# A two-layer decoder trunk on one core: four heads' values of one attention run in a row with the next four heads' scores, their results in the sums' banks, the second attention two units sooner

## The chip, the cores and the metric

The kernel runs on one core of one Trainium2 chip. A core has a matrix engine (TensorE, PE in the profile; its weight loads are listed as PEld), VectorE (DVE), ScalarE (ACT), GpSimd (POOL) and a queue engine (SyncE, SP), which here issues nearly all transfers. TensorE writes to PSUM, an accumulator memory of eight banks of 128 partitions by 512 float32; ScalarE and VectorE read it from there into SBUF. The metric is the device time of one execution in microseconds. Before the change it is 841.62 us, the median of three runs (841.48 to 841.85).

## The reference

The input is `x` of 1 x 256 x 1024 in float32, through two layers and a final RMSNorm. A layer adds a mixer of three gated branches and then a squared-ReLU MLP:

```
h = rms_norm(x, attn_norm[l])
p = h @ w_in                      # split into cq, ckv, k_rope, mq, mk, mv, rq, rk, rv, rg, three gates
o_mla  = mla_branch(...)          # 8 heads, causal attention, head size 96 for scores and 64 for values
o_moba = moba_branch(...)         # 8 heads of 64; one block of 256 keys, so it is causal attention too
o_ret  = retention_branch(...)    # 4 heads, decay matrix, group norm, silu(g)
merged = sigmoid(g_mla) * (o_mla @ w_branch_mla) + ... + sigmoid(g_ret) * (o_ret @ w_branch_ret)
x = x + merged @ w_out
x = x + square(relu(rms_norm(x, mlp_norm[l]) @ w_mlp_up)) @ w_mlp_down
```

Each attention head needs scores of 256 queries by 256 keys, a softmax over the causal part, and the product of the probabilities with the values.

## The kernel before

**Products.** The weights arrive as float32 in pieces of up to 128 x 1024. `fetch` (L180) lets ScalarE round each piece to a high part `whi` (L191) and VectorE form the rest `wlo` (L193); activations are split in the same way. A product is the sum of three matmuls, `three` (L211 to L214), each with 128 x 512 results as a rule. The attention's own products take unsplit float32, which the profile shows as two matmul records each.

**Units and steps.** The work of a layer's mixer is a list `prog` of units, most of them 24 matmuls with one piece pair of weights: `project` (L324) makes four units for each 512 columns of `w_in`, and `branch` (L487) four units for each branch's output product. `at(slot, step)` hangs a small step (transposes, scores, values) behind a unit. Counted from the unit "mv 3", which is 0, the units are: gate of MLA 1 to 8, gate of MoBA 9 to 16, MLA's output product 17 to 20, `rqk` 21 to 24, `rv` 25 to 28, `rg` 29 to 32, MoBA's output product 33 to 36, then the retention's gate.

**The first attention (MLA).** Its heads' scores (L750) stand at units 0 to 7, one head a unit, the turning of the probabilities (`turn`, L419: three transposes into `ps_pt`, and a ScalarE copy to `probT`) two units later, and `values` (L437) for heads 0 to 3 at unit 6 and for heads 4 to 7 at unit 10.

**The second attention (MoBA).** `first` is unit 12 (L762). `moba_turn` (L766) transposes two heads' queries and keys into `pqk`, which ScalarE copies (`copied_pair`, L384). `four` (L464) makes four heads' scores by `together` (L373) and their softmax, at units 12 and 21 (`GAP` is 9); the turning stands 3 and 4 units behind that, `values` 5 units behind, at 17 and 26.

**Parts of the array.** A head of the second attention has 64 rows, so `together` gives two heads to the two halves of the array's rows (tile 64 x 128 in the profile: `64*128`). `values` gives two heads to the two halves of the columns (`128*64`). The retention's scores (`ret_scores`, L812, unit 28) run through `together` as well, behind `ret_turn` (L802, units 26 and 27). All other matmuls take the whole array (`128*128`).

**Banks.** PSUM has four banks under the tag `acc`, for the sums of projections and branches (two at a time), and four under `misc` for all else, among them `values`' result `po`, which `split_plain` (L230) reads by ScalarE (high part) and VectorE (low part).

**Order.** Each engine runs its list strictly in order and waits at semaphores. The lists are written at build time by a planner that runs the program in a timing model of its own and moves instructions of one engine past each other where data allow. Only inside `tc.manual_schedule(engines={PE})` the written order of TensorE's instructions holds among themselves. In the kernel before, `together` and `values` have such a block each.

Of the kernel before, what the change touches and what calls it, by code (L numbers as in the profile page):

```python
# [7 lines left out]
F32 = mybir.dt.float32  # L8
# [6 lines left out]
P = 128  # L15
D = 1024
S = 256
# [111 lines left out]
def trunk(ctx: ExitStack, tc: tile.TileContext, gx, wts, consts, gfin, gn, xtok, out):  # L129


    nc = tc.nc
# [4 lines left out]
    sb = ctx.enter_context(tc.tile_pool(name="sb", bufs=1))  # L137
# [8 lines left out]
    DEC = cp.tile([P, K_END - K_DEC], F32, name="DEC")  # L146
# [55 lines left out]
    def misc_tile(name="misc"):  # L202
        return ps.tile([P, 512], F32, name=name, tag="misc", bufs=4)
# [4 lines left out]
    def t4(name):  # L208
        return sb.tile([P, 4, S], F32R, name=name, tag="t4", bufs=T4)
# [20 lines left out]
    def split_plain(src, hi, lo):  # L230
        nc.scalar.activation(hi, src, AF.Copy)
        nc.vector.tensor_sub(lo, src, hi.bitcast(F32))
# [126 lines left out]
    def rope(xv, c0, s0, t, n, h, w=None):  # L359
# [10 lines left out]
        nc.vector.tensor_sub(xv[:, :, 0, :], av[:, :, 0, :], bv[:, :, 1, :])  # L370
        nc.vector.tensor_add(xv[:, :, 1, :], av[:, :, 1, :], bv[:, :, 0, :])

    def together(parts, heads):  # L373

        with tc.manual_schedule(engines={mybir.EngineType.PE}):
            for banks, a, b in heads:
                for o, sa, sb_ in parts:
                    for j, bank in enumerate(banks):  # L380
                        rows = slice(64 * j, 64 * j + 64)
                        nc.tensor.matmul(bank[:, o], a[rows, sa], b[rows, sb_], start=True, stop=True)  # L382

    def copied_pair(pt):  # L384

# [4 lines left out]
    def attention_head(score, scale):  # L390


        got = {}

        def scores(s_ps=None):
            if s_ps is None:
                s_ps = misc_tile("ps_s")
                score(s_ps[:, 0:P], slice(0, P), slice(0, P))
                score(s_ps[:, P : 3 * P], slice(P, S), slice(0, S))
            p = sb.tile([P, 3 * P], F32, name="prob", bufs=4)  # L400
            m = small("smx")
# [12 lines left out]
            nc.vector.reciprocal(m[:, 6:8], m[:, 4:6])  # L414
            for i, (a, b) in enumerate(spans):
                nc.vector.tensor_scalar(p[:, a:b], p[:, a:b], m[:, 6 + i : 7 + i], None, op0=ALU.mult)
            got["p"] = p

        def turn():  # L419
            pt = misc_tile("ps_pt")  # L420
            for i, src in enumerate((0, P, 2 * P)):
                nc.tensor.transpose(pt[:, P * i : P * i + P], got["p"][:, src : src + P], ident)  # L422
            pT = sb.tile([P, 3 * P], F32, name="probT", bufs=5)
            nc.scalar.activation(pT, pt[:, : 3 * P], AF.Copy)
            return pT

        return scores, turn

    def attention(oT, score, vs, scale, first, group=None):


        pT = {}

        def turned(h, turn):
            pT[h] = turn()

        def values(h0):  # L437


            o, v = misc_tile("po"), vs()  # L440
            with tc.manual_schedule(engines={mybir.EngineType.PE}):
                for h in (h0 + 2, h0):
                    cs = slice(S * (h - h0) // 2, S * (h - h0) // 2 + S)
                    for i in range(2):
                        for j in (1, 0):
                            vh = v[i][:, VD * (h + j) : VD * (h + j) + VD]
                            dst = o[64 * j : 64 * j + 64, cs]
                            if i == 0:
                                nc.tensor.matmul(dst, vh, pT[h + j][:, 0:S], start=True, stop=False)  # L449
                            else:  # L450
                                nc.tensor.matmul(dst[:, P:S], vh, pT[h + j][:, S : 3 * P], start=False, stop=True)  # L451
            split_plain(o, *(part[:, h0 // 2 : h0 // 2 + 2, :].rearrange("p k s -> p (k s)") for part in oT))

        heads = [attention_head(lambda o, qs, ks, h=h: score(h, o, qs, ks), scale) for h in range(8)]
        for h, (scores, turn) in enumerate(heads):
            if group is None:
                at(first + h, scores)
                at(first + h + 2, lambda h=h, turn=turn: turned(h, turn))
                if h % 4 == 3:
                    at(first + h + 3, lambda h=h: values(h - 3))  # L460
        if group is None:
            return

        def four(h0):  # L464
            for h, bank in enumerate(group(h0), h0):
                heads[h][0](bank)

        for i in range(2):
            at(first + GAP * i, lambda i=i: four(4 * i))
            for h in range(4):  # L470
                at(first + GAP * i + 3 + h // 2, lambda h=4 * i + h: turned(h, heads[h][1]))
            at(first + GAP * i + 5, lambda i=i: values(4 * i))

    def gates(l, key, xn):

# [98 lines left out]
    def layer(l, xn, before):  # L574

        c0 = []
        c, mla, mqkv, rqkv = {}, {}, {}, {}
# [164 lines left out]
        omlaT, omobaT, oretT = [], [], []  # L742
# [9 lines left out]
        attention(  # L752
            omlaT, mla_score,
            lambda: mla["v"], QKD**-0.5, first,
        )

        th_moba = gates(l, "gmoba", xn)
        merged, mT = {}, ([], [])  # L760
        branch(l, "bmla", omlaT, th_mla, merged)
        first = slot("gmoba0", 3)  # L762
        at(first, lambda: omobaT.extend((t4("omobah"), t4("omobal"))))
        qkT = {}

        def moba_turn(i):  # L766
            pt = misc_tile("pqk")
            for a, key in enumerate(("mq", "mk")):
                for t in range(NT):
                    nc.tensor.transpose(  # L770
                        pt[:, (2 * a + t) * P : (2 * a + t + 1) * P], mqkv[key][t][:, P * i : P * i + P], ident
                    )
            qkT[i] = copied_pair(pt)
# [8 lines left out]

        for i in range(4):
            at(first + 4 * (i // 2) - 3 + i % 2, lambda i=i: moba_turn(i))
        attention(omobaT, None, lambda: mqkv["mv"], MB_D**-0.5, first, moba_scores)

# [13 lines left out]
        rT, or_ps, aT, rg, oret = [], [], {}, {}, []  # L800

        def ret_turn(i):  # L802
            pt = misc_tile("prt")
            for a in range(2):
                for t in range(NT):
                    nc.tensor.transpose(
                        pt[:, (2 * a + t) * P : (2 * a + t + 1) * P],
                        rqkv["rqk"][t][:, 256 * a + P * i : 256 * a + P * i + P], ident,
                    )
            rT.append(copied_pair(pt))  # L810

        def ret_scores():  # L812
            banks = [misc_tile("ps_r") for _ in range(RT_H)][::-1]
            together(
                ((slice(0, S), slice(0, P), slice(0, S)), (slice(S, 3 * P), slice(P, S), slice(P, S))),
                [(banks[2 * i : 2 * i + 2], rT[i][1], rT[i][0]) for i in range(2)],
            )
            for h in range(RT_H):
                aT[h] = sb.tile([P, 3 * P], F32, name="retA", tag="prob", bufs=4)
                nc.vector.tensor_mul(aT[h], banks[h][:, : 3 * P], DEC[:, 384 * h : 384 * h + 384])  # L820

        def ret_values(h):
            if h == 0:
# [259 lines left out]
        for t in range(NT):  # L1083
# [3 lines left out]
            for half in range(2):  # L1087
                cs = slice(512 * half, 512 * half + 512)
# [35 lines left out]
FIRST = 4  # L1124
WHOLE = 1
AHEAD = 1
GAP = 9
T4 = 9


# [73 lines left out]
```

## Time and profile before

| What | Value |
|---|---|
| median of three runs | 841.62 us |
| the profiled execution itself | 841.8 us, its span 840.0 us |
| TensorE matmuls | 833.3 us busy, 99% of the span, 4454 records |
| VectorE | 575.0 us, 68% |
| ScalarE | 491.4 us, 59% |
| GpSimd | 27.9 us, 3% |
| DMA | 151.10 MB, 180 GB/s on the mean |

A matmul's row in the timeline has its start, its duration, line and tiles. Matmuls overlap in the pipeline, so a row lasts longer than the time to the next start, and what one costs is read from start to start; of a row that merges several records only the first start is shown. Times in the timeline count from the start of the span.

### The profile page before, as it was taken

Reading aid. Unit: us, or ns where it says so; the run is one execution under the profiler, and the core shown is the slowest. Engines: PE = TensorE matmul, PEld = TensorE weight load, DVE = VectorE, ACT = ScalarE, POOL = GpSimd, SP = SyncE. Lnnn points to the kernel's source line nnn. Section 1 sums busy time; section 2 is a strip of 40 time slices with the busy share of each in tenths; the row PEclk is TensorE's granted clock in tenths of the full one; section 3 lists DMA queues with packets and bytes.
Section 4 is the critical chain, followed back from the end, with each engine's and each line's share of the span. In section 5 each row is a group of like instructions: output and inputs, shape, how many; then the busy total and the mean of one; then the engine's idle time right before and its main releaser. Section 6 shows DMA issues by size and latency. Waiting matters only on the chain.

```text
span 840.0 us, 12183 instructions
## 1 busy us (share of the span) xinstructions
PE 833.3 (99%) x4454; PEld 708.6 (84%) x4454; DVE 575.0 (68%) x1088; ACT 491.4 (59%) x860; POOL 27.9 (3%) x31
## 2 busy tenths in 40 slices
PE   9999999999999999999999999999999999999997
PEld 7888877888998888888888887788889988888886
DVE  6887568596777666666589865675968666666663
ACT  7757666445556555555677666564556555555552
POOL 0000000040000000000000000001300000000000
PEclk9999999999999999999999999999999999999999
DMA  9755544546456665656366545554665556666641
GB/s 343 272 202 185 175 136 147 160 131 215 144 177 222 199 190 190 194 187 190 114 212 211 178 137 174 148 159 145 178 207 165 170 187 197 200 185 193 194 130 51
DMA packets 43115, 151.10 MB, mean 180 GB/s; under 512 B 4912, under 2 KB 5936, under 8 KB 43056
## 3 DMA queue, kind: packets, MB, share of 16 engines
q1 hardware_dynamic: 42480, 149.66, 56.4%
q8 instruction: 35, 0.57, 0.3%
q10 hardware_dynamic: 576, 0.67, 0.2%
q14 instruction: 24, 0.20, 0.1%
HBM read 149.26 MB, written 1.05 MB: 179 GB/s over the span
## 4 chain that ended last, share of the span: by engine, by line
PE 99%; DVE 0%; ACT 0%; issue 0%; DVEq 0%
PE acc L212 20%; PE acc L214 20%; PE acc L213 20%; PE pup L979 13%; PE pup L981 7%; PE acc L930 5%; PE ps_pt L422 1%; PE ps_s L750 1%; PE po L449 1%; PE ps_s L382 1%; PE acc L643 1%; PE acc L644 0%; PE pqk L770 0%; PE acc L646 0%; PE warm L554 0%; PE po L451 0%
## 5 line engine op out<-in xcount | busy, mean ns | idle before, releaser
L193 DVE TENSOR_TENSOR wlo<-raw,whi 128x1024 fp32r<-128x1024 f32 (+4 forms) x287 | 337.9, 1185 | 192.4 <-ACT whi L191 134.8
L191 ACT ACTIVATE whi<-raw 128x1024 fp32r<-128x1024 f32 (+4 forms) x287 | 292.3, 1023 | 188.2 <-PE acc L214 101.3
L212 PE MATMUL acc<-whi,xs 128*128 128x512 f32 (+1 forms) x384 | 151.8, 397 | 0.0
L213 PE MATMUL acc<-wlo,xs 128*128 128x512 f32 (+1 forms) x384 | 150.5, 392 | 0.0
L214 PE MATMUL acc<-whi,xs 128*128 128x512 f32 (+1 forms) x384 | 149.5, 390 | 0.0
L979 PE MATMUL pup<-xs,whi 128*128 128x512 f32 x496 | 121.3, 390 | 0.0
L979 PEld LDWEIGHTS pup<-xs,whi 128*128 128x128 f32 x496 | 92.4, 188 | 18.8
L212 PE MATMUL acc<-whi,sq 128*128 128x512 f32 x256 | 100.1, 391 | 0.0
L213 PE MATMUL acc<-wlo,sq 128*128 128x512 f32 x256 | 99.9, 390 | 0.0
L214 PE MATMUL acc<-whi,sq 128*128 128x512 f32 x256 | 99.0, 389 | 0.0
L212 PEld LDWEIGHTS acc<-whi,xs 128*128 128x128 f32 x384 | 72.1, 188 | 15.2 <-issue 1.3
L214 PEld LDWEIGHTS acc<-whi,xs 128*128 128x128 f32 x384 | 72.1, 188 | 14.3
L213 PEld LDWEIGHTS acc<-wlo,xs 128*128 128x128 f32 x384 | 72.2, 188 | 13.4
L981 PE MATMUL pup<-xs,wlo 128*128 128x256 f32 x496 | 68.3, 283 | 0.0
L981 PEld LDWEIGHTS pup<-xs,wlo 128*128 128x128 f32 x496 | 65.6, 191 | 2.8
L990 ACT ACTIVATE relu<-relu 128x256 f32<-128x256 f32 x64 | 25.8, 410 | 57.1 <-DVE relu L989 57.1
L214 PEld LDWEIGHTS acc<-whi,sq 128*128 128x128 f32 x256 | 48.0, 188 | 10.1
L212 PEld LDWEIGHTS acc<-whi,sq 128*128 128x128 f32 x256 | 48.2, 188 | 9.3
L213 PEld LDWEIGHTS acc<-wlo,sq 128*128 128x128 f32 x256 | 48.2, 188 | 9.0
L411 ACT ACTIVATE prob<-prob,smx 128x128 f32<-128x128 f32 x64 | 28.4, 446 | 15.5 <-DVE smx L408 15.1
L930 PE MATMUL acc<-mTh,whi 128*128 128x256 f32 x128 | 32.0, 285 | 0.0
L930 PE MATMUL acc<-mTh,wlo 128*128 128x256 f32 x128 | 31.7, 283 | 0.0
(247 smaller groups left out, 1035.9 us busy)
## 6 DMA issues: line engine op xcount, KB each, us to landing
raw<-wts SPq DMA_DIRECT2D x264, 512.0 KB, 4.0
raw<-wts SPq DMA_DIRECT2D x6, 464.0 KB, 7.8
raw<-wts SPq DMA_DIRECT2D x4, 416.0 KB, 3.2
xrow<-xtok SPq DMA_DIRECT2D x4, 256.0 KB, 8.1
gn<-gn SPq DMA_DIRECT2D x2, 512.0 KB, 4.1
raw<-wts SPq DMA_DIRECT2D x3, 256.0 KB, 4.0
DEC<-consts SPq DMA_DIRECT2D x1, 768.0 KB, 6.0
y<-y SPq DMA_DIRECT2D x2, 352.0 KB, 2.6
```

Of the source, the lines that this page charges most:

```text
L191: nc.scalar.activation(hi[:, cs], raw[:, cs], AF.Copy)
L193: nc.vector.tensor_sub(lo[:, cs], raw[:, cs], hi[:, cs].bitcast(F32))
L212: nc.tensor.matmul(o, ah, bh, start=start, stop=False)
L213: nc.tensor.matmul(o, ah, bl, start=False, stop=False)
L214: nc.tensor.matmul(o, al, bh, start=False, stop=stop)
L382: nc.tensor.matmul(bank[:, o], a[rows, sa], b[rows, sb_], start=True, stop=True)
L411: nc.scalar.activation(p[:, a:b], p[:, a:b], AF.Exp, bias=m[:, 2 + i : 3 + i], scale=scale, accum_out=m[:, 4 + i : 5 + i])
L422: nc.tensor.transpose(pt[:, P * i : P * i + P], got["p"][:, src : src + P], ident)
L930: nc.tensor.matmul(acc[:, :S], a, b, start=i == 0 and ks[0] == 0, stop=i == len(jobs) - 1 and ks[-1] == KD - 1)
L979: nc.tensor.matmul(u, w, xm.both(k), start=k == 0, stop=False)
L981: nc.tensor.matmul(u[:, 0:S], w, xm.k(k)[0], start=False, stop=k == KD - 1)
L990: nc.scalar.activation(s, s, AF.Square)
```

## The change

- A new helper, `in_a_row`, calls several jobs inside one block of fixed TensorE order, and then runs what each of them returns: the work of the other engines.
- `values` and the scores' jobs no longer open a block of their own. They return their ScalarE and VectorE work as a function.
- The first attention's values of heads 4 to 7 run in one block with the second attention's scores of heads 0 to 3 (unit 10). The second attention's values of heads 0 to 3 run with its scores of heads 4 to 7 (unit 18), and its values of heads 4 to 7 run behind the retention's scores (unit 28). The first attention's values of heads 0 to 3 stay by themselves (unit 6).
- Those three results `po` take a bank of the tag `acc`; the one that stands alone stays in `misc`.
- The second attention begins at unit 10 and no longer at 12, and `GAP` is 8 and no longer 9, so its second four heads' scores stand at unit 18 and no longer at 21. The transposes of its queries and keys move with it, from units 9, 10, 13 and 14 to 7, 8, 11 and 12.
- The retention's scores take their second pair of heads first.

```
+    def in_a_row(*jobs):
+        with tc.manual_schedule(engines={mybir.EngineType.PE}):
+            rest = [job() for job in jobs]
+        for job in rest:
+            job()
+
     def together(parts, heads):
-        with tc.manual_schedule(engines={mybir.EngineType.PE}):
-            for banks, a, b in heads:
...
+        for banks, a, b in heads:
...
-        def values(h0):
-            o, v = misc_tile("po"), vs()
-            with tc.manual_schedule(engines={mybir.EngineType.PE}):
-                for h in (h0 + 2, h0):
...
-            split_plain(o, *(part[:, h0 // 2 : h0 // 2 + 2, :].rearrange("p k s -> p (k s)") for part in oT))
+        def values(h0, bank=acc_tile):
+            o, v = bank("po"), vs()
+            for h in (h0 + 2, h0):
...
+            dst = (part[:, h0 // 2 : h0 // 2 + 2, :].rearrange("p k s -> p (k s)") for part in oT)
+            return lambda: split_plain(o, *dst)
...
-                if h % 4 == 3:
-                    at(first + h + 3, lambda h=h: values(h - 3))
-        if group is None:
-            return
+            at(first + 6, lambda: in_a_row(lambda: values(0, misc_tile)))
+            return lambda: values(4)
 
         def four(h0):
-            for h, bank in enumerate(group(h0), h0):
-                heads[h][0](bank)
+            banks = group(h0)
+            def rest():
+                for h, bank in enumerate(banks, h0):
+                    heads[h][0](bank)
+            return rest
 
+        at(first, lambda: in_a_row(former, lambda: four(0)))
+        at(first + GAP, lambda: in_a_row(lambda: values(0), lambda: four(4)))
         for i in range(2):
-            at(first + GAP * i, lambda i=i: four(4 * i))
             for h in range(4):
                 at(first + GAP * i + 3 + h // 2, lambda h=4 * i + h: turned(h, heads[h][1]))
-            at(first + GAP * i + 5, lambda i=i: values(4 * i))
+        return lambda: values(4)
...
-        first = slot("gmoba0", 3)
+        first = slot("gmoba0", 1)
...
-                [(banks[2 * i : 2 * i + 2], rT[i][1], rT[i][0]) for i in range(2)],
+                [(banks[2 * i : 2 * i + 2], rT[i][1], rT[i][0]) for i in (1, 0)],
...
-        at(slot("rv", 3), ret_scores)
+        at(slot("rv", 3), lambda: in_a_row(ret_scores, moba_last))
...
-GAP = 9
+GAP = 8
```

More of the change, by code (lines that the diff above doesn't have):

```diff
@@ L371, in rope @@
         nc.vector.tensor_add(xv[:, :, 1, :], av[:, :, 1, :], bv[:, :, 0, :])
-    def together(parts, heads):
-        with tc.manual_schedule(engines={mybir.EngineType.PE}):
-            for banks, a, b in heads:
[L379 to L382, printed above, removed]
+    def in_a_row(*jobs):
[3 more added lines that the diff above has]
+            job()
+    def together(parts, heads):
+        for banks, a, b in heads:
+            for o, sa, sb_ in parts:
+                for j, bank in enumerate(banks):
+                    rows = slice(64 * j, 64 * j + 64)
+                    nc.tensor.matmul(bank[:, o], a[rows, sa], b[rows, sb_], start=True, stop=True)
     def copied_pair(pt):
@@ L427, in attention_head, with attention @@
         return scores, turn
-    def attention(oT, score, vs, scale, first, group=None):
+    def attention(oT, score, vs, scale, first, group=None, former=None):
         pT = {}
@@ L435, in turned @@
             pT[h] = turn()
-        def values(h0):
-            o, v = misc_tile("po"), vs()
-            with tc.manual_schedule(engines={mybir.EngineType.PE}):
-                for h in (h0 + 2, h0):
[L443 to L451, printed above, removed]
-            split_plain(o, *(part[:, h0 // 2 : h0 // 2 + 2, :].rearrange("p k s -> p (k s)") for part in oT))
+        def values(h0, bank=acc_tile):
+            o, v = bank("po"), vs()
+            for h in (h0 + 2, h0):
+                cs = slice(S * (h - h0) // 2, S * (h - h0) // 2 + S)
+                for i in range(2):
+                    for j in (1, 0):
+                        vh = v[i][:, VD * (h + j) : VD * (h + j) + VD]
+                        dst = o[64 * j : 64 * j + 64, cs]
+                        if i == 0:
+                            nc.tensor.matmul(dst, vh, pT[h + j][:, 0:S], start=True, stop=False)
+                        else:
+                            nc.tensor.matmul(dst[:, P:S], vh, pT[h + j][:, S : 3 * P], start=False, stop=True)
+            dst = (part[:, h0 // 2 : h0 // 2 + 2, :].rearrange("p k s -> p (k s)") for part in oT)
+            return lambda: split_plain(o, *dst)
@@ L454, in attention @@
         heads = [attention_head(lambda o, qs, ks, h=h: score(h, o, qs, ks), scale) for h in range(8)]
-        for h, (scores, turn) in enumerate(heads):
-            if group is None:
+        if group is None:
+            for h, (scores, turn) in enumerate(heads):
                 at(first + h, scores)
                 at(first + h + 2, lambda h=h, turn=turn: turned(h, turn))
-                if h % 4 == 3:
-                    at(first + h + 3, lambda h=h: values(h - 3))
-        if group is None:
-            return
+            at(first + 6, lambda: in_a_row(lambda: values(0, misc_tile)))
+            return lambda: values(4)
@@ L750, in mla_score @@
             nc.tensor.matmul(o, mla["Q"][:, h, qs], mla["K"][:, h, ks], start=True, stop=True)
[L752 to L755, printed above, removed]
+        mla_last = attention(omlaT, mla_score, lambda: mla["v"], QKD**-0.5, first)
         th_moba = gates(l, "gmoba", xn)
@@ L784, in layer @@
             at(first + 4 * (i // 2) - 3 + i % 2, lambda i=i: moba_turn(i))
-        attention(omobaT, None, lambda: mqkv["mv"], MB_D**-0.5, first, moba_scores)
+        moba_last = attention(omobaT, None, lambda: mqkv["mv"], MB_D**-0.5, first, moba_scores, mla_last)
         def ret_done(key):
@@ L815, in ret_scores, with rest @@
                 ((slice(0, S), slice(0, P), slice(0, S)), (slice(S, 3 * P), slice(P, S), slice(P, S))),
-                [(banks[2 * i : 2 * i + 2], rT[i][1], rT[i][0]) for i in range(2)],
+                [(banks[2 * i : 2 * i + 2], rT[i][1], rT[i][0]) for i in (1, 0)],
             )
-            for h in range(RT_H):
-                aT[h] = sb.tile([P, 3 * P], F32, name="retA", tag="prob", bufs=4)
-                nc.vector.tensor_mul(aT[h], banks[h][:, : 3 * P], DEC[:, 384 * h : 384 * h + 384])
+            def rest():
+                for h in range(RT_H):
+                    aT[h] = sb.tile([P, 3 * P], F32, name="retA", tag="prob", bufs=4)
+                    nc.vector.tensor_mul(aT[h], banks[h][:, : 3 * P], DEC[:, 384 * h : 384 * h + 384])
+            return rest
         def ret_values(h):
```

## The prediction

> **What bounds the kernel now.** I read the first part of the page (busy time by engine) and the chain that ended last, then the waits of TensorE, and after that the timeline of TensorE and of ScalarE around the attentions.
>
> ```profile
> PE 833.3 (99%) x4454; PEld 708.6 (84%) x4454; DVE 575.0 (68%) x1088; ACT 491.4 (59%) x860; POOL 27.9 (3%) x31
> ...
> PE 99%; DVE 0%; ACT 0%; issue 0%; DVEq 0%
> ```
>
> ```profile
> PE warm L554 <- PEq L1197: 0.8, 1, 0.8
> ```
>
> TensorE is the chain, and its only wait of the whole span is the 0.8 us at the start. So the time is the sum of TensorE's steps from start to start. A change gains only where a step becomes shorter, and any new wait of TensorE is paid in full.
>
> The steps that change are those at a switch between the whole array and a half. First a stretch of four heads' values (columns) between projection matmuls, then one that ends at transposes, then row stretches of two and of four heads' scores, all from TensorE's timeline:
>
> ```profile
> 125.59 0.39 PE L212 MATMUL acc<-whi,omlah 128*128 128x512 f32 x1
> 125.82 0.39 PE L213 MATMUL acc<-wlo,omlah 128*128 128x512 f32 x1
> 126.14 0.65 PE L449 MATMUL po<-probT,mv 128*64 128x256 f32 x4
> 126.62 0.39 PE L451 MATMUL po<-probT,mv 128*64 128x128 f32 x4
> 126.84 0.60 PE L449 MATMUL po<-probT,mv 128*64 128x256 f32 x4
> 127.27 0.39 PE L451 MATMUL po<-probT,mv 128*64 128x128 f32 x4
> 127.59 0.50 PE L214 MATMUL acc<-whi,omlal 128*128 128x512 f32 x1
> 127.92 0.40 PE L212 MATMUL acc<-whi,omlah 128*128 128x512 f32 x1
> ```
>
> ```profile
> 106.10 0.39 PE L451 MATMUL po<-probT,vml 128*64 128x128 f32 x4
> 106.42 0.44 PE L770 MATMUL pqk<-K,mq 128*128 128x128 f32 x2
> 106.69 0.38 PE L770 MATMUL pqk<-K,mk 128*128 128x128 f32 x2
> 107.00 0.93 PE L382 MATMUL ps_s<-qkT 64*128 64x128 f32 x8
> 107.86 0.50 PE L212 MATMUL acc<-whi,xs 128*128 128x512 f32 x1
> ...
> 131.12 0.39 PE L214 MATMUL acc<-whi,xs 128*128 128x512 f32 x1
> 131.44 1.58 PE L382 MATMUL ps_s<-qkT 64*128 64x128 f32 x16
> 132.95 0.50 PE L212 MATMUL acc<-whi,xs 128*128 128x512 f32 x1
> 133.28 0.40 PE L213 MATMUL acc<-wlo,xs 128*128 128x512 f32 x1
> ...
> 152.54 1.09 PE L806 MATMUL prt<-K,rqk 128*128 128x128 f32 x8
> ...
> 155.09 0.39 PE L214 MATMUL acc<-whi,xs 128*128 128x512 f32 x1
> ...
> 155.78 0.39 PE L214 MATMUL acc<-whi,xs 128*128 128x512 f32 x1
> ...
> 158.14 1.58 PE L382 MATMUL ps_r<-qkT 64*128 64x256 f32 x16
> ```
>
> A whole-array step is 0.23 us (125.59 to 125.82). **Columns:** the step in takes 0.32 (+0.09); the two halves of the stretch compare as 0.48 against 0.43 (+0.05, just after the switch) and 0.22 against 0.32 (+0.10, the step out); the matmul after that takes 0.33 (+0.10). That is 0.14 in and 0.20 out, 0.34 in all. Out to transposes it is +0.10 (106.10 to 106.42) and +0.05 (two transposes in 0.27, where their step is 0.11: eight in 1.09 less the last one's own 0.27), together 0.15. **Rows:** eight records take 0.86 and sixteen 1.51, so eight records without a switch are 0.65, and 0.21 belongs to the two ends, 0.11 behind the way in and 0.10 for the way out. The step in is +0.09 (131.12 to 131.44; from the second transpose at 106.80 to 107.00 it is 0.20 against 0.11), the matmul behind it +0.10. That is 0.20 in and 0.20 out, 0.40 in all; out to transposes again 0.15.
>
> **The change part by part.** Terms 1 to 3 make the sum.
>
> **1. Fewer stretches.** In the order of the built program, a layer before has eight of them: three column stretches that end at transposes (0.29 each: 0.14 in, 0.15 out), one between projections (0.34), and four row stretches, since the first scores of the second attention stand as two pairs of heads apart: three at 0.40 and the second pair at 0.35, which ends at transposes. The sum is 0.87 + 0.34 + 1.20 + 0.35 = 2.76 us. After, it has four: one values stretch alone (0.29), two of values and then scores (0.14 in, 0.20 out), and one of the retention's scores and then values (0.20 in, 0.20 out). Without the inner switches that is 0.29 + 0.68 + 0.40 = 1.37, a gain of 1.39 us a layer. No row of before has a switch from columns to rows. If it costs nothing the gain is 1.39. If it costs a way out of one half shape (0.10) and the step behind the way into the other (0.11 for rows, 0.05 for columns), the three cost 0.21 + 0.21 + 0.15 = 0.57, and the gain is 0.82. If it costs a full way out and a full way in (0.34 to 0.40), the three cost 1.1 and the gain is 0.3. I take 0.57: every switch in the rows, in or out, of either shape, next to projections or to transposes, costs 0.14 to 0.20, and an inner switch at 0.15 to 0.21 is the value nearest to them. Two layers: **-1.6 us**, between -2.8 and -0.6.
>
> [...]
>
> **2. A new wait at the retention's scores.** Before, the eight transposes `prt` ran at 152.54 and the scores `ps_r` at 158.14, and ScalarE had 5 us for the copies between:
>
> ```profile
> 152.66 0.60 ACT L231 ACTIVATE omobah<-po 128x512 fp32r<-128x512 f32 x1 [0.58 <-PE po L451]
> 153.23 1.07 ACT L387 COPY qkT<-prt 128x512 f32<-128x512 f32 x2
> 155.52 1.38 ACT L793 ACTIVATE rv<-acc,ms 128x512 f32<-128x512 f32 x2 [1.21 <-PE acc L214]
> 156.80 1.05 ACT L191 ACTIVATE whi<-raw 128x1024 fp32r<-128x1024 f32 x1
> ```
>
> In the changed program's order the planner has put six of the eight transposes behind the last matmul of unit "rv 3", and the fixed block of `ps_r` and `po` directly behind them, in both layers. ScalarE's list has at that place: two `rv` copies, one `whi` of 128 x 1024, and only then the two `qkT` copies that `ps_r` reads. ScalarE takes them strictly in that order. Call L the start of the unit's last matmul (155.78 before). The first `rv` copy starts at L - 0.26 and both last 1.38, to L + 1.12; `whi` starts 0.10 before that end and lasts 1.05, to L + 2.07; the two copies start 0.10 earlier and last 1.07, to L + 3.04, and 0.04 more for the signal (0.04 is from the bank's end at 155.09 + 0.39 to 155.52). TensorE would be ready at L + 0.23 + 5 x 0.11 + 0.20 = L + 0.98. It waits 3.08 - 0.98 = 2.1 us. Nothing can cover that: all of TensorE's later work is queued behind it. Two layers: **+4.2 us**. The ends: if the `whi` were not ahead, 1.15 a layer; if one more such piece were, 3.1.
>
> Who waits behind it: VectorE's decay products, whose readers stand 36 matmuls (8.2 us) later, and the split of `po`, whose reader is unit 33. Neither comes late.
>
> **3. A short wait in layer 0 at unit 10.** There the order has head 7's transposes, three matmuls, and then `values`, which begins with head 7.
>
> ```profile
> L424 ACT ACTIVATE probT<-ps_pt 128x384 f32<-128x384 f32 x32 | 14.6, 486 | 7.3 <-PE ps_pt L422 7.3
> L481 ACT ACTIVATE th<-acc,half 128x512 f32<-128x512 f32 x24 | 16.2, 686 | 5.5 <-PE acc L214 5.4
> L511 DVE SCALAR_TENSOR_TENSOR th<-th,acc 128x512 f32<-128x512 f32 x8 | 5.3, 681 | 0.5 <-PE acc L214 0.5
> ```
>
> From the first transpose to `values` TensorE needs 3 x 0.11 + 3 x 0.23 + 0.09 = 1.1 us. ScalarE has a gate's 0.69 ahead of the copy of 0.49; the gate's bank is ready 0.39 - 0.23 + 0.04 = 0.2 us after that transpose, and 0.2 + 0.69 - 0.10 + 0.49 + 0.04 = 1.3. **+0.2 us**, between 0 and 0.3. In layer 1 eighteen matmuls (4.1 us) stand there, and nothing waits.
>
> **4. What costs nothing.** `po` in the `acc` banks: a project holds two of the four, and the next two are asked for at units 13, 19 and 29. The tight place is unit 19, right behind unit 18's stretch: but that stretch has 1.3 us of values and 1.3 of scores, time for the two products of 0.68 that free the branch's banks. If VectorE came late there, one piece more would be at most 0.7 a layer. The second attention's transposes, softmax and copies move by two or three units as a whole; VectorE and ScalarE are idle 32% and 41% of the span, and the same instructions run. The lists of SP and POOL hold the same transfers and operations; only the load `gn` goes behind four weight pieces in SP's list, still units ahead of its reader at unit 32.
>
> **The sum:** -1.6 + 4.2 + 0.2 = +2.8 us on the profiled execution's 841.8 us (span 840.0), that is 844.6. That execution stands 0.2 above the median of 841.62, so I forecast 844.4.
>
> **The rivals.** *Inner switches are free.* For it: steps between the two halves of one shape cost nothing. Against it: all switches seen cost. -2.8 + 4.4 = +1.6, 843.2, inside what a measurement can tell from no change (0.2% of 841.62, 1.7 us).
>
> *The wait at `ps_r` isn't there* (the other side): ScalarE reaches the `qkT` copies before the `rv` copies, as it did before at 153.23. 841.6 - 1.6 + 0.2 = 840.2, or 839.0 with free switches. It decides once the wait is below 0.7 us a layer, a third of what I reckon. Against it: the order of both lists is fixed at build time, and ScalarE can't pass over the `rv` copies, which need the unit's last matmuls.
>
> *The wait lowers TensorE's clock.* The start of the span shows a slow state:
>
> ```profile
> 0.77 3.57 PE L554 MATMUL warm<-const-bfloat16-1.0 128*128 128x512 bf16 x8 [0.77 <-PEq L1197]
> ...
> 5.23 0.41 PE L643 MATMUL acc<-whi,xs 128*128 128x256 f32 x1
> 5.45 0.41 PE L644 MATMUL acc<-whi,xs 128*128 128x256 f32 x1
> ...
> 5.87 0.41 PE L644 MATMUL acc<-whi,xs 128*128 128x256 f32 x1
> 6.09 0.44 PE L643 MATMUL b<-whi,xs 128*128 128x416 f32 x1
> ```
>
> A step of 256 columns is 0.22 us there, as long as a 512's 0.23 later on, and that lasts until 6.1 us, from a first matmul at 0.8. If each 2.1 us wait brought this back for 5 us, 2.5 us would be lost each: 849.4. Nothing in the span after the start shows it, but no pause of TensorE is there either. [...]
>
> **How the numbers follow.** Forecast 0.72 (its own range 843.6 to 845.4), free switches 0.13, no wait or a short one 0.09 (half of it faster by over 0.2%, half within), clock 0.06. So faster 0.05, same 0.17, slower 0.78. The range goes from 842.9, below the free switches, to 845.9, where the inner switches cost a full way out and in (841.6 - 0.6 + 4.4 = 845.4) and VectorE adds 0.5; it leaves out the clock and the missing wait.
>
> **What would show it.** Right: four half-array stretches a layer; two waits of about 2.1 us of `ps_r` on the ScalarE `qkT` copy, near 155 and 570 us, and a short one of the first `po` with `mv`'s scores behind it near 99; inner steps of some 0.2 from `po` to `ps_s`, where 0.10 would say that they are free. Wrong: `ps_r` without idle time before it, or steps of 0.4 behind the wait. A wait at the first matmuls of unit 19 would say that the banks weren't free.

## The result, and the profile after

The changed kernel takes 846.21 us (median of six executions, 843.67 to 846.49), the kernel before 841.36 beside it (840.99 to 841.85). The ratio over the executions is 1.0048 (95% interval 1.0037 to 1.0059), that of the two medians alone 1.0058. So it is slower, as forecast, but the median lies 1.8 us above the forecast of 844.4 and 0.3 us above the end of the range.

The six times are not one group. Two are 843.67 and 844.09, four lie between 846.18 and 846.49, and nothing is in between; what tells the two groups apart is a main finding below.

The profiled execution is one of the upper group, 846.49 us with a span of 844.7. The busy time by engine and the chain that ended last, of the changed kernel:

```profile
PE 833.8 (99%) x4454; PEld 710.5 (84%) x4454; DVE 574.5 (68%) x1088; ACT 490.0 (58%) x860; POOL 28.1 (3%) x31
...
PE 98%; ACT 1%; issue 0%; DVE 0%; DVEq 0%
```

TensorE is as busy as before, and 1% of the chain, of which ScalarE had 0% before, now belongs to ScalarE. The waits of TensorE (us in total, times, longest) name it:

```profile
PE ps_r L389 <- ACT qkT L394: 4.1, 2, 2.0
PE warm L567 <- PEq L1211: 0.8, 1, 0.8
```

TensorE's timeline at the retention's scores, layer 0 and then layer 1 (start, duration, line, tiles; in brackets the idle time before):

```profile
153.41 0.39 PE L214 MATMUL acc<-whi,xs 128*128 128x512 f32 x1
153.65 0.81 PE L816 MATMUL prt<-K,rqk 128*128 128x128 f32 x6
156.49 2.54 PE L389 MATMUL ps_r<-qkT 64*128 64x256 f32 x16 [2.03 <-ACT qkT L394]
158.96 1.12 PE L456 MATMUL po<-probT,mv 128*64 128x256 f32 x4
...
161.07 0.50 PE L212 MATMUL acc<-whi,xs 128*128 128x512 f32 x1
...
571.10 0.82 PE L816 MATMUL prt<-K,rqk 128*128 128x128 f32 x6
573.94 1.58 PE L389 MATMUL ps_r<-qkT 64*128 64x256 f32 x16 [2.03 <-ACT qkT L394]
575.45 0.65 PE L456 MATMUL po<-probT,mv 128*64 128x256 f32 x4
575.93 0.39 PE L458 MATMUL po<-probT,mv 128*64 128x128 f32 x4
...
576.90 0.50 PE L212 MATMUL acc<-whi,xs 128*128 128x512 f32 x1
```

ScalarE in the same stretch of layer 0:

```profile
153.16 1.38 ACT L803 ACTIVATE rv<-acc,ms 128x512 f32<-128x512 f32 x2 [1.13 <-PE acc L214]
154.43 1.05 ACT L191 ACTIVATE whi<-raw 128x1024 fp32r<-128x1024 f32 x1
155.38 1.06 ACT L394 COPY qkT<-prt 128x512 f32<-128x512 f32 x2
```

The wait has the order that was forecast, `rv`, `rv`, `whi`, and only then the two `qkT` copies, which end at 156.44; the scores start at 156.49, which is 3.08 behind the unit's last matmul at 153.41.

But the two layers differ behind the wait. The sixteen `ps_r` take 158.96 - 156.49 = 2.47 us in layer 0 and 575.45 - 573.94 = 1.51 in layer 1; the values behind them take 2.11 and 1.45. Layer 0 loses 0.96 + 0.66 = 1.6 us there. The granted clock in windows of the span says why (a row gives the length, then busy time and count of PE, PEld, DVE, ACT and POOL, the granted clock, the share of the DMA engines, GB/s):

```profile
153.50:156.90 3.40, 1.37 (x12) 1.02 (x12) 1.23 (x1) 2.94 (x5) 0.00 (x0) 1.00 0.51 161
157.00:160.30 3.30, 3.30 (x24) 2.45 (x24) 1.25 (x3) 0.00 (x0) 0.00 (x0) 0.50 0.48 161
160.40:163.80 3.40, 3.40 (x22) 2.60 (x19) 1.29 (x3) 0.60 (x1) 0.00 (x0) 1.00 0.02 5
...
573.40:576.70 3.30, 2.76 (x32) 2.26 (x32) 1.94 (x4) 0.49 (x2) 0.00 (x0) 1.00 0.50 149
```

In layer 0 TensorE runs at half clock from 157.0 to 160.3, directly behind the wait; in layer 1, behind a wait of the same length, the clock stays at 1.00.

Next come the short wait in layer 0 and the inner switch from columns to rows, again from TensorE's timeline:

```profile
99.35 0.40 PE L214 MATMUL acc<-whi,xs 128*128 128x512 f32 x1
99.87 0.65 PE L456 MATMUL po<-probT,vml 128*64 128x256 f32 x4
...
101.00 0.39 PE L458 MATMUL po<-probT,vml 128*64 128x128 f32 x4
101.32 1.58 PE L389 MATMUL ps_s<-qkT 64*128 64x128 f32 x16
102.83 0.50 PE L212 MATMUL acc<-whi,xs 128*128 128x512 f32 x1
```

The step into the values is 0.52 where it was 0.32: 0.20 us of wait. From the last group of values to the scores it is 0.32, where such a group takes 0.22 inside the values, and the sixteen scores take 1.51, as they do behind projection matmuls.

Three marks that both kernels have show where the time went: the same scores of the first attention, ahead of anything that the change touches, and the first and last matmul of the MLPs. Before, and then after:

```profile
69.94 0.82 PE L750 MATMUL ps_s<-KK,Q 128*128 128x128 f32 x4
...
L979 PE MATMUL pup<-xs,whi x496: 389/389/481, 240.6 to 818.9; 128*128 128x512 f32 x166
```

```profile
70.32 0.82 PE L763 MATMUL ps_s<-KK,Q 128*128 128x128 f32 x4
...
L993 PE MATMUL pup<-xs,whi x496: 389/389/481, 244.1 to 823.7; 128*128 128x512 f32 x166
```

| Part of the span | Difference | Made of |
|---|---|---|
| start, up to the first mark | +0.4 | 70.32 - 69.94; nothing is changed there |
| layer 0's mixer | +3.1 | 3.5 - 0.4; the waits 2.03 and 0.20, the half clock 1.6, so -0.7 is left for the stretches |
| layer 1's mixer | +1.3 | 4.8 - 3.5; the wait 2.03, so -0.7 is left for the stretches |
| together | +4.8 | the span alone: 840.0 to 844.7, +4.7 |

### The profile page after: what moved, and what is told of

Same layout as the page of the kernel before. It is cut to its first block, busy times and chain, and to the rows that moved or that the text cites. A ratio compares the mean times of both kernels' runs of the same rounds, so it can differ in the third digit from the quotient of the medians.

```text
span 844.7 us, 12182 instructions
## 1 busy us (share of the span) xinstructions
PE 833.8 (99%) x4454; PEld 710.5 (84%) x4454; DVE 574.5 (68%) x1088; ACT 490.0 (58%) x860; POOL 28.1 (3%) x31
## 3 DMA queue, kind: packets, MB, share of 16 engines
HBM read 149.26 MB, written 1.05 MB: 178 GB/s over the span
## 4 chain that ended last, share of the span: by engine, by line
PE 98%; ACT 1%; issue 0%; DVE 0%; DVEq 0%
PE acc L212 20%; PE acc L214 20%; PE acc L213 20%; PE pup L993 13%; PE pup L995 7%; PE acc L944 5%; PE ps_s L763 1%; PE ps_pt L429 1%; PE po L456 1%; PE ps_s L389 1%; PE acc L656 1%; PE acc L657 0%; PE ps_r L389 0%; PE acc L659 0%; PE po L458 0%; PE warm L567 0%
```

## The experiments

Each diff is against the changed kernel, and each ratio is to the kernel before, run beside it.

**The retention's row one unit later.** If the wait comes from ScalarE's list, 24 more matmuls ahead of the row must take it away.

```
-        at(slot("rv", 3), lambda: in_a_row(ret_scores, moba_last))
+        at(slot("rg", 0), lambda: in_a_row(ret_scores, moba_last))
```

> Edit: the row of the retention's scores and the second attention's last four values stands one unit later (behind the first unit of rg and not behind the last of rv); all rows and banks stay as in the changed kernel. Theory W (the whole loss is TensorE's wait for the two qkT copies, 2.1 us a layer, and what it does to the clock): no wait of ps_r, the clock at 1.00 throughout, the same four half-array stretches a layer, 841.4 - 1.6 + 0.2 = 840.0 us, between 839.6 and 840.4, all runs within 0.6 us of each other. Rival S (the stretches in a row or the moved second attention cost it): 843.5 us or more, as the changed kernel.

Measured: 840.34 us (839.56 to 840.69, 11 executions), ratio 0.9982 (0.9974 to 0.9991): faster than before. TensorE's only listed wait is the 0.8 us at the start. ScalarE's list at that place is the same, but now there is time for it:

```profile
152.83 1.38 ACT L803 ACTIVATE rv<-acc,ms 128x512 f32<-128x512 f32 x2 [1.13 <-PE acc L214]
154.11 1.05 ACT L191 ACTIVATE whi<-raw 128x1024 fp32r<-128x1024 f32 x1
155.06 1.07 ACT L394 COPY qkT<-prt 128x512 f32<-128x512 f32 x2
```

```profile
160.44 1.58 PE L389 MATMUL ps_r<-qkT 64*128 64x256 f32 x16
```

The copies end at 156.1 and the scores start at 160.44. So one unit of distance was all that the row lacked, and what is left of the change is the gain of the stretches less the short wait, together about 1.5 us.

**The retention's copies by VectorE.** This takes away ScalarE's list as the cause and leaves the row where it is.

```
-    def copied_pair(pt):
+    def copied_pair(pt, copy=None):
...
-        nc.scalar.copy(o, pt)
+        (copy or nc.scalar.copy)(o, pt)
...
-            rT.append(copied_pair(pt))
+            rT.append(copied_pair(pt, nc.vector.tensor_copy))
```

> Edit: the two copies of the retention's transposes run on VectorE and not on ScalarE, everything else as in the changed kernel. VectorE's list has one wlo of 1.2 us ahead of them, which needs the whi, so the wait of ps_r becomes about 1.1 us a layer and no longer 2.1. Theory W: 841.4 - 1.6 + 0.2 + 2.2 = 842.2 us (841.6 to 842.6). [...]

Measured: 842.39 us (842.03 to 842.73, 11 executions), ratio 1.0008 (0.9999 to 1.0017). The wait is halved and has another releaser:

```profile
PE ps_r L389 <- DVE qkT L394: 2.1, 2, 1.1
```

All eleven executions lie within 0.7 us, so with waits of 1.05 us there is one group.

**Each retention copy made twice.** `prt` is copied by ScalarE into a scratch tile first and from there to `qkT`, so the wait grows by the two extra copies.

```
-            rT.append(copied_pair(pt))
+            twice = sb.tile([P, 2 * S], F32, name="twice", bufs=1)
+            nc.scalar.copy(twice, pt)
+            rT.append(copied_pair(twice))
```

> Edit: each retention transpose is copied twice on ScalarE, one after the other, which adds two copies of 0.6 us to the chain before ps_r in each layer; all else as in the changed kernel. Theory W: the wait is 3.5 us a layer and no longer 2.1, so 841.4 - 1.6 + 0.2 + 7.0 = 847.0 us without a drop of the clock. [...] Rival R (a drop is chance at any pause, as in four of six runs so far): runs spread between 847 and 851.

Measured: 851.6 us (848.79 to 852.96, five executions), ratio 1.0115 (1.0099 to 1.0130). The waits are 3.46 us each, and behind them, in windows of the span:

```profile
PE ps_r L389 <- ACT qkT L394: 6.9, 2, 3.5
```

```profile
158.00:161.30 3.30, 3.30 (x24) 2.24 (x20) 1.95 (x4) 0.00 (x0) 0.00 (x0) 0.50 0.16 63
...
574.40:577.70 3.30, 1.90 (x12) 1.64 (x14) 0.22 (x1) 1.29 (x3) 0.00 (x0) 0.50 0.51 158
577.80:581.10 3.30, 3.30 (x24) 2.22 (x20) 1.95 (x4) 0.00 (x0) 0.00 (x0) 0.50 0.00 0
```

The half clock now comes with both waits: 3.4 us of it behind the first, and 6.7 us from 574.4 on, where the second wait has 1.4 us to go (TensorE is busy for 1.90 of the row's 3.30 us). Without it the two waits, 2 x 1.43 us longer, would give some 846.5 to 847.0 from the changed kernel's lower group; the executions lie 2 to 6 us above that, and the five differ by 4 us among themselves. All five lie above the 847.0 that was worked out without a drop of the clock, three of them above 851 as well. The fastest, 848.79, has a listed mean clock of 0.997, the other four have 0.991 to 0.993, which fits one half-clock stretch of 3.4 us in it and several in the others; only the profiled one's trace shows them.

**The changed kernel once more.** Are the two groups there again?

> The changed kernel again. [...]

Measured: 843.69, 843.80, 843.81, 846.13 and 846.44 us, ratio 1.0036 (1.0023 to 1.0049). With the first six, five executions lie in 843.67 to 844.09 and six in 846.13 to 846.49. This time the profiled execution is of the lower group (843.69):

```profile
PE ps_r L389 <- ACT qkT L394: 4.1, 2, 2.0
...
PE warm L567 <- PEq L1211: 0.8, 1, 0.8
```

```profile
69.18 0.82 PE L763 MATMUL ps_s<-KK,Q 128*128 128x128 f32 x4
...
L993 PE MATMUL pup<-xs,whi x496: 389/389/481, 241.3 to 820.9; 128*128 128x512 f32 x166
```

The waits are the same, so the groups don't differ in them. The two profiled executions differ by 846.49 - 843.69 = 2.80 us: 70.32 - 69.18 = 1.14 of it arises before the first mark, and 1.6 is the half clock of layer 0. Against before, the two mixers cost 1.5 and 1.3 here; less the waits of 2.23 and 2.03, the stretches give -0.7 a layer, as in the other execution.

**Only the retention's row kept.** The other two rows and the second attention's earlier place are undone.

```
-        at(first, lambda: in_a_row(former, lambda: four(0)))
-        at(first + GAP, lambda: in_a_row(lambda: values(0), lambda: four(4)))
+        at(first - 2, lambda: in_a_row(former))
+        at(first, lambda: in_a_row(lambda: four(0)))
+        at(first + GAP, lambda: in_a_row(lambda: four(4)))
+        at(first + 5, lambda: in_a_row(lambda: values(0)))
...
-        first = slot("gmoba0", 1)
+        first = slot("gmoba0", 3)
...
-GAP = 8
+GAP = 9
```

> Only the retention's scores and the last values stay in a row; the other two rows are undone and the second attention begins at unit 12 again, with 9 units between its halves. What this tells: whether the 2.0 us wait belongs to the retention's row by itself, or to that row together with the second attention's earlier place. If the row alone makes the wait, ps_r waits some 2.0 us in each layer as in the changed kernel, and the time is about 841.6 - 0.5 (the stretches that this row saves) + 4.2 = 845.3, with the half clock in some executions. If the wait needs the order that the earlier place brings about (the qkT copies behind the two rv copies and the whi piece in ScalarE's list), there is no wait at ps_r; in the list of this kernel the copies stand ahead of them. Then the only wait is one of about 1 us at the values in layer 0, and the time is 841.8 + 1.0 - 0.7 = 842.1. I expect the second.

Measured: 842.08 us (841.68 to 842.56, 11 executions), ratio 1.0006 (0.9997 to 1.0015). No wait at `ps_r`; ScalarE's copies come ahead of the `rv` copies again, and the one new wait is the 0.9 us at the values in layer 0:

```profile
PE po L456 <- ACT probT L431: 0.9, 1, 0.9
```

```profile
153.39 1.07 ACT L394 COPY qkT<-prt 128x512 f32<-128x512 f32 x2 [0.48 <-PE prt L818]
154.64 1.38 ACT L805 ACTIVATE rv<-acc,ms 128x512 f32<-128x512 f32 x2 [0.17 <-PE acc L214]
```

So the row by itself doesn't make the 2.0 us wait: it takes the row and the order that the planner writes when the second attention stands earlier. (The rows are undone in the program; in layer 1 the planner set values and scores side by side even so, at 514.43 and 515.88.)

**All rows, the second attention two units later.**

```
-        first = slot("gmoba0", 1)
+        first = slot("gmoba0", 3)
```

> All rows kept, but the second attention begins at unit 12 as before, 8 units between its halves. By the order of the lists, two waits are left at ps_r of about 0.5 us each, and one of about 1.0 us at the values beside the scores in layer 0, near 99 us. The stretches save about 1.6 us as in the changed kernel. By the theory that only the waits and the stretches count: 841.8 - 1.6 + 2.0 = 842.2. By the rival that the second attention's earlier place itself costs nothing and the rows cost more than I reckon: 844 or more. The clock: 1.0 us of idle time is below the 1.63 us that made no drop so far, so all executions should lie in one group within 0.5 us and at a granted clock of 0.999.

Measured: 842.03 us (841.49 to 842.48, 11 executions), ratio 1.0003 (0.9994 to 1.0012), in one group. The waits are 0.90 us at `po` in layer 0 and 0.38 at each `ps_r`:

```profile
PE po L456 <- ACT probT L431: 0.9, 1, 0.9
...
PE ps_r L389 <- ACT qkT L394: 0.8, 2, 0.4
```

Without the earlier place the gain of the rows and the short waits cancel, and in layer 0 the first row came apart in the built order, its values at 99.97 and its scores at 103.71. The earlier place shortens the wait of the first attention's values (0.9 down to 0.2 us) and costs the retention's scores 2 x 1.65.

**The results back in the misc banks.**

```
-        def values(h0, bank=acc_tile):
+        def values(h0, bank=misc_tile):
```

> The results po go to the misc banks again, all else as in the changed kernel. If the sums' banks did nothing but give po a free bank (my step 4), the time is that of the changed kernel: 843.8 without a drop of the clock, 846.2 with. By the built order the banks decide more: po can't have a misc bank while the scores hold them, so the rows break up again into seven stretches a layer, the qkT copies come ahead, and no wait is left at ps_r: 841.8 - 0.8 = 841.0, one group, no drop of the clock. I expect the second, 841.0 (840.3 to 841.7).

Measured: 843.10 us (842.89 to 843.47, 11 executions), ratio 1.0019 (1.0010 to 1.0027). This is a miss by 2.1 us. The mechanism is there: no wait at `ps_r`, one group, and the rows break up: `po` now takes one of the four misc banks, of which four heads' scores need all four. The price of a broken row was too small. One piece of ten scores and the other of six, 4.6 us later:

```profile
126.48 1.14 PE L389 MATMUL ps_s<-qkT 64*128 64x128 f32 x10
127.55 0.50 PE L213 MATMUL acc<-wlo,omlah 128*128 128x512 f32 x1
...
132.12 0.92 PE L389 MATMUL ps_s<-qkT 64*128 64x128 f32 x6
132.97 0.50 PE L214 MATMUL acc<-whi,xs 128*128 128x512 f32 x1
```

They take 1.07 + 0.85 = 1.92 us where sixteen in one piece take 1.51, and there is one more way in and one more slow matmul behind (0.09 + 0.10): a break costs 0.6, and I had taken 0.4 for one more stretch. Four breaks, two in each layer, explain 0.8 of the 2.1. Another 0.8 the expectation had left out: it counted seven stretches in place of eight, 0.4 saved a layer, and gave no price to the inner switches from values to scores, of which this kernel keeps two a layer (4 x 0.21). About 0.5 stays open. The banks part of the change thus moved no wait by itself, but it is what lets the rows stand whole.

**Three rows.** The retention's row one unit later, and the first attention's values of heads 0 to 3, the last stretch that stood alone, in the row at unit 10. It needs eight `probT` buffers.

```
-            pT = sb.tile([P, 3 * P], F32, name="probT", bufs=5)
+            pT = sb.tile([P, 3 * P], F32, name="probT", bufs=8)
...
-            at(first + 6, lambda: in_a_row(lambda: values(0, misc_tile)))
-            return lambda: values(4)
+            return lambda: (lambda done: (lambda: [d() for d in done]))([values(4), values(0)])
...
-        at(slot("rv", 3), lambda: in_a_row(ret_scores, moba_last))
+        at(slot("rg", 0), lambda: in_a_row(ret_scores, moba_last))
```

> The retention's row one unit later (as in the first experiment, where the wait at ps_r was gone), and the values of the first attention's heads 0 to 3, which stood alone at unit 6, behind those of heads 4 to 7 in the row at unit 10. Three half-array stretches a layer are left. By the step model (a stretch of columns between projections and transposes 0.29, taken away in each layer) it saves 0.6 us beside the first experiment's 840.3 (1.5 below before) and has no wait: 839.7, or 2.1 below before. If the extra column stretch inside the row costs as much as a stretch by itself, 840.3 as in the first experiment. If the sums' bank that the second po takes holds up the next project, a wait shows at the first matmuls of unit 11 or 12, and the time is above 840.3.

Measured: 839.48 us (839.34 to 840.32, ten executions), ratio 0.9975 (0.9966 to 0.9984). This is the fastest kernel of the study, 2.2 us below before, with no wait of TensorE listed but the start's.

**The wait filled with work.** Do the two groups come from TensorE's idle time? Constant matmuls in bf16 are put into the wait, into a bank that the scores overwrite; eight of them in one kernel, one in the other.

```
             banks = [misc_tile("ps_r") for _ in range(RT_H)][::-1]
+            for i in range(8):
+                nc.tensor.matmul(
+                    banks[3], nc.const_aps.tensor(1.0, [P, P], BF16), nc.const_aps.tensor(1.0, [P, 512], BF16), start=True, stop=True
+                )
```

> The changed kernel with eight matmuls of 128 x 512 in bf16 on constants put ahead of the retention's scores in each layer, into a bank that these scores then overwrite. They stand in the 2.0 us in which TensorE waits for the qkT copies, and take about 8 x 0.22 = 1.8 us of it, so that the scores start when they started before: 0.2 to 0.3 us of idle time is left there. By the theory that the two groups of the changed kernel's executions (843.7 to 844.1 and 846.1 to 846.5) come from TensorE's idle time and its clock, all executions now lie in the lower group, 843.6 to 844.4, at a granted clock of 0.998 or 0.999. By the rival that the groups come from something else in those executions (transfers, the start), about half still lie above 846.

Measured: 844.34 us (844.29 to 844.59, six executions), ratio 1.0032 (1.0020 to 1.0045). The scores start as late as ever, 2.85 us behind the transposes' start (2.84 before the fill), but TensorE is idle for only 0.28 of it, and no execution is above 844.6 (843.6 to 844.4 had been expected):

```profile
153.17 0.82 PE L816 MATMUL prt<-K,rqk 128*128 128x128 f32 x6
153.83 1.91 PE L825 MATMUL ps_r<-const-bfloat16-1.0 128*128 128x512 bf16 x8
156.02 1.58 PE L389 MATMUL ps_r<-qkT 64*128 64x256 f32 x16 [0.28 <-ACT qkT L394]
```

> The same with one such matmul instead of eight: it runs at the front of the wait and leaves some 1.75 us of idle time behind it, between the 1.63 us of one window that made no drop of the clock and the 2.00 us that made one. If the bound lies near 1.7 or below, the two groups stay as in the changed kernel, 843.7 to 844.1 and 846.1 to 846.5. If it lies above 1.75, all executions are in the lower group. I lean to the second, since three quarters of the waits of 2.0 us made no drop: 60 to 40.

Measured: 844.25 us (843.68 to 844.53, six executions), ratio 1.0031 (1.0019 to 1.0042). One matmul leaves 1.81 us of idle time, and the upper group is gone as well. In layer 1 the idle time lies whole within the first row below (3.30 - 1.49 = 1.81), and the clock behind it stays at 1.00:

```profile
PE ps_r L389 <- ACT qkT L394: 3.6, 2, 1.8
```

```profile
568.70:572.00 3.30, 1.49 (x12) 0.97 (x10) 1.08 (x2) 3.23 (x5) 0.00 (x0) 1.00 0.65 205
572.10:575.40 3.30, 3.30 (x34) 2.59 (x35) 1.94 (x5) 0.34 (x1) 0.00 (x0) 1.00 0.49 164
```

Had the upper group kept its share of the changed kernel (6 of 11), twelve executions in a row without one would be a chance of less than one in a thousand; the six with one matmul by themselves, about one in a hundred. The changed kernel itself did not run beside these twelve. So the upper group goes with a wait of 2.0 us in which TensorE has nothing to do, and in these six executions 0.2 us less of it was enough to be rid of it.

## Why the prediction was right and wrong

**1. Fewer stretches: right.** -0.7 a layer in both profiled executions of the changed kernel against -0.8 taken. The value of 0.57 for the three inner switches holds in its parts: from columns to rows 0.10 on the step and 0.11 more over the scores (record by record, the step from the last `po` to the first `ps_s` is the 0.20 that the prediction named as its sign), from rows to columns 0.05 on the values behind (575.45 to 575.93, 0.48, against 0.43) and 0.10 ahead of them. The rival of free switches falls: it needed -1.4. The first experiment, where this term and the short wait are left, gives 840.34 against the 840.2 that was worked out for a kernel without the wait.

**2. The wait at the retention's scores: right**, 2.03 us in each layer for 2.1. The first two experiments show the cause from both sides, later scores and another copying engine. The fifth adds what the prediction had read off the built order but not told apart: the row alone doesn't make it.

**3. The short wait at unit 10: right**, 0.20 us.

**4. What costs nothing: right for the changed kernel.** No wait at the first matmuls of unit 19 nor anywhere else. It was too narrow a reading of the banks, as the misc kernel showed: they cost nothing and they keep the rows whole.

**The sum without the clock** is therefore met: 843.67 to 844.09 in five of eleven executions, 0.3 to 0.7 below 844.4. That difference can be the start: in the profiled execution of this group the first mark stands 0.76 earlier than in that of before (69.18 against 69.94), which is no part of the change.

**The rivals: here it failed**, in the third, "The wait lowers TensorE's clock", which had 0.06 and was left out of the range. The prediction set it aside with "Nothing in the span after the start shows it, but no pause of TensorE is there either". That is not so: at the end of the span of before, TensorE's last matmul ends at 834.05, and the granted clock is half from 839.12 on, 5.1 us later. That costs nothing there, but it is half clock behind idle time. The 0.06 was the author's estimate; no run of then had a wait of this length. The trace of the changed kernel shows half clock behind one wait of 2.03 us and full clock behind the other. Six of eleven executions lie in the upper group, so it decides the median: about 2.3 us between the groups, 1.6 of it at half clock behind the wait in the execution whose trace shows it. The rival's own price was wrong too. It took 5 us of half clock behind each wait, 2.5 us lost each; in the trace it was 3.41 us behind one wait, 1.6 lost. A range that counts on a single such loss would have had to reach 846.0 at least (844.4 + 1.6).

The side was right, slower at 0.78, and for the reason given: the lower group, without the half clock, is slower than before as well. How far the median lies from the forecast is chance: with one of the six upper executions in the lower group, the median of the eleven would have lain near 844.

## What to carry to other kernels

When instructions are fixed in a row on the engine that bounds, look up what the first of them reads and where that stands in the other engine's list: here three pieces of 0.7 to 1 us stood ahead, and one unit more of distance turned +0.5% into -0.2%. Price a new wait of TensorE as its length, and look at the granted clock behind it: here one of four traced waits of 2.0 us had 3.41 us of half clock behind it, 1.6 us lost. If such a wait can't be removed, a dummy matmul at its front can be worth trying: here one left 1.81 us, and none of six executions was in the upper group. Two groups of times with nothing between are a reason to look at the granted clock behind each wait, in an execution of each group.

## What the runs showed of the hardware

**Some waits of TensorE have half clock behind them.** In the profiled execution of the changed kernel the trace's records of the granted clock stand at 6.74 us (full for the first time), 156.93 (half), 160.34 (full) and 843.01 (half). So there is one half-clock stretch inside the work, 3.41 us long, and it begins 0.44 us behind the end of layer 0's wait at 156.49. The last record stands 4.2 us behind the end of the last matmul at 838.78. With each copy made twice, the rows from 157.9 to 161.3 and from 574.4 to 581.1 are at 0.50, 3.4 and 6.7 us.

| Wait at `ps_r`, us | Granted clock behind it | Run |
|---|---|---|
| 3.46 | half for 3.4 us | copies twice, layer 0 |
| 3.46 | half for 6.7 us, the first 1.4 of it still in the wait | copies twice, layer 1 |
| 2.03 | half for 3.41 us, the sixteen `ps_r` in 2.47 us | changed kernel, layer 0 |
| 2.03 | full, 1.51 us | changed kernel, layer 1 |
| 2.03 | full, 1.50 us | changed kernel again, layer 0 |
| 2.0 | full, 1.00 in the row behind | changed kernel again, layer 1 |
| 1.81 | full, 1.51 us | one matmul as fill, layer 0 |
| 1.81 | full, 1.00 in the row behind | one matmul as fill, layer 1 |
| 0.28 | full, 1.00 | eight matmuls as fill, both layers |

**The length of the wait alone doesn't sort them.** 2.03 us stands on both sides, and in one execution. Nor does TensorE's idle time in a row of the profile ahead of the clock's reading. The 1.63 and 2.00 us of the expectations are the idle time of such stretches, in the rows below 3.30 - 1.72 = 1.58 and 3.40 - 1.45 = 1.95; first the changed kernel again, then copies twice, layer 1 of each:

```profile
567.40:570.70 3.30, 1.72 (x11) 1.26 (x9) 1.07 (x2) 2.89 (x5) 0.00 (x0) 1.00 0.77 246
570.80:574.10 3.30, 2.96 (x32) 2.29 (x32) 1.94 (x4) 0.29 (x1) 0.00 (x0) 1.00 0.62 175
```

```profile
570.90:574.30 3.40, 1.45 (x10) 1.03 (x8) 1.18 (x2) 3.23 (x5) 0.00 (x0) 1.00 0.68 208
574.40:577.70 3.30, 1.90 (x12) 1.64 (x14) 0.22 (x1) 1.29 (x3) 0.00 (x0) 0.50 0.51 158
```

Against them stands layer 1 of the changed kernel, with 3.40 - 1.41 = 1.99 us idle and full clock behind:

```profile
570.50:573.90 3.40, 1.41 (x10) 1.00 (x8) 1.18 (x2) 3.28 (x5) 0.00 (x0) 1.00 0.76 229
573.90:577.40 3.50, 3.46 (x34) 2.75 (x35) 2.13 (x5) 0.38 (x1) 0.00 (x0) 1.00 0.50 155
```

So a bound on the idle time was not shown, nor why equal waits in equal executions differ.

**The start differs too.** In the upper execution 9 matmuls fall into 0.8 to 4.1 us and 15 into 4.2 to 7.5, in the lower one 8 and 22. If the lower one reaches its full pace near 4.2 us and the upper at 6.74, some 2.5 us at half pace cost 1.3 us, an estimate from these counts and that record, near the other 1.14 between the two profiled ones.

Open: one of the six upper executions, 846.44, has a listed mean clock of 0.999, as the lower ones have, where the others have 0.996 or 0.997. A stretch of 3.41 us at half clock alone takes 0.002 off the mean, so the figure speaks against one in that execution, and no trace of it is there to decide. Nor is the clock behind the wait the only thing that can cost 2 us: one of 32 executions of the kernel before, which has no such wait, took 844.01 us.
